# Delta-net: weight loads and splits at a higher priority than the small steps around them

## The chip, the cores and the metric

The kernel runs on one core of a Trainium2 chip. The metric is the device time of one execution in microseconds (us); of several executions the median is taken. The core's engines are PE (TensorE, the matrix products), DVE (VectorE), ACT (ScalarE) and POOL (GpSimd); SP issues the DMAs and works as a queue. PE loads its weights in instructions of their own (PEld) beside the products. TensorE's clock has two levels here, 1.2 and 2.4 GHz; a granted clock of 0.50 in the profile is the lower of them.

## What is computed

One inference step of a trunk of two layers, for 512 tokens of a new prompt and 8 x 4 tokens of samples with a state, 544 columns together, at a width of 1024. Layer 0 mixes by an mLSTM, layer 1 by a gated delta rule, and behind each mixer stands an MLP with a squared ReLU:

```python
for layer in range(DEPTH):                       # 2
    if layer % N_MIXERS == 0:
        y, Cj, nj, mj = mlstm_mixer(x, a_w_in[j], ...)
    else:
        y, Sj, cj = gdn_mixer(x, b_w_in[j], b_conv_w[j], ..., b_w_out[j], S[j], conv[j])
    x = layer_norm(ALPHA * x + y, ln1_g[layer], ln1_b[layer])
    x = layer_norm(ALPHA * x + sq_relu_mlp(x, mlp_w1[layer], mlp_w2[layer]), ...)
```

The change bears on the delta-net mixer:

```python
proj = x @ w_in                                  # 1024 -> 6176 columns
c = silu(conv(proj[..., :CONV_DIM]))             # 4 taps; q, k of 8 heads, v of 16
q = l2norm(q) * DK_B ** -0.5;  k = l2norm(k)
A = M + I                                        # triangle of each head and chunk
sol = triangular_solve(A, rhs)                   # u, w
for each chunk:                                  # the scan, state S
    v_new = u - w @ S;  o = qg @ S + attn @ v_new
    S = gL * S + kdec.T @ v_new
o = head_rms(o) * norm_w * silu(z)
y = o @ w_out                                    # 2048 -> 1024
```

## The kernel before

Activations lie transposed, as tiles of 128 features by 544 columns, in two halves of 272 (`HS`). A weight comes as a tile of 128 outputs: `load_w` takes a raw tile (`wraw`, 128 x 1024, f32, 512 KB), issues its DMA on SP's queue, takes the tiles `wh` and `wl`, and lets `split` make the high part on ACT (a cast, L110) and the low part on DVE (a subtraction, L111). `mm3` multiplies: for each of the 8 blocks k of 128 inputs three products of 128 x 272 in L191, high by high, high by low (`XL`), low (`wl`) by high. The third one of a block is the first to need `wl`. Of `wraw`, `wh` and `wl` there are two buffers each, so the DMA of a tile waits until the split of the tile two before it has read its buffer.

The order of work on every engine is set at build time: each instruction gets a priority when the program text issues it, and among those that are ready with their buffers the scheduler takes the one with the earlier priority. `tc.high_priority(offset=n)` gives the instructions within it a priority n places earlier. Each engine, and SP's queue, then runs its list strictly in order.

The delta-net stage lies at some 690 to 1435 us of the trace. Its weight products run in the sequence `ORDER = "p0 p1 p2 p3 y0 w0 p4 p5 y1 w1 p6 p7 y2 w2 y3 w3"`. A p is `project` for one unit (one head of q and k, two of v): four weight tiles of `wb`, convolution (`conv`: `acc` and `pre`, L983 to L1007, with a sigmoid chain, L507 to L510), transposes and norms. A y is `gate_out` for four heads (`wb` again; the result, split, is `gyh`, `gyl`), a w is the output product with the tiles of `wbo`.

The small work runs beside it in three lanes, each a list of Python generators. `mm3` calls `tick()` behind each block k, and a lane whose period is over makes one step, so that its instructions are issued between products:

- `lane_i`, for each unit: `prepare` makes the triangles (`U`, `A`; L1082 to L1108), brings their 16 x 16 diagonal blocks through DRAM (`dg`, `ub`; L1112, L1117), inverts these on DVE in fifteen steps of two instructions (`tb`, `xb`; L1125, L1127), and sends them back (`dx`, `xc`; L1130, L1132). `invert` builds the inverse of 128 x 128 from them: `DT` (L1156), then short products on PE with an ACT or DVE step behind each (L1164, L1171, L1185, L1193 and L1196, L1205, L1211).
- `lane_s`, the scan over four chunks of 128 tokens (L1243 to L1288), once the inverse is there.
- `lane_d`, for each pair of units the samples: `decode` with the state's tiles `sst` (loads L1294, products of 128 x 8 in L1368), and `update` (products L1419, DVE L1424, stores L1425).

`lanes` is filled at the start of the stage and emptied by `lanes.clear()` at its end; in all other stages it is an empty list.

Of the kernel before, what the change touches and what calls it, by code (L numbers as in the profile page):

```python
# [33 lines left out]
NEG = -1e30  # L34
CLAMP = -40.0
HP = 400
BANKS = (3, 2, 2, 1)
NST = 2
NOT = 6
# [31 lines left out]
def hybrid_kernel(  # L71
# [27 lines left out]
    dma = nc.sync.dma_start  # L99
# [6 lines left out]
    def r32(ap):  # L106
        return ap.bitcast(F32)

    def split(hi, lo, src):
        S.copy(hi, src)  # L110
        V.tensor_tensor(lo, src, r32(hi), op=ALU.subtract)  # L111

    def mtile(tag="a"):
        return pm.tile([P, 512], F32, tag=tag, name="pm_" + tag, bufs=BANKS["gast".index(tag)])

    wide, once = [], []

    def gtile():
# [7 lines left out]
        if tag != "g":  # L126
            return mtile(tag)[:, :HN]
        return pg.tile([P, 512], F32, tag="g", name="pg_t", bufs=BANKS[0])[:, :HN]

# [29 lines left out]
    lanes, done = [], set()  # L159
# [12 lines left out]
    def load_w(src, alloc=None):  # L172

        wn[0] += 1
        pool = wx[0] if wx[0] is not None and wn[0] % 2 else wp
        raw = pool.tile([P, KD, P], F32, tag="wraw", name="wraw", bufs=WBUFS[0])
        dma(raw, src)
        if alloc is None:
            wh = wp.tile([P, KD, P], F32R, tag="wh", name="wh", bufs=WBUFS[1])
            wl = wp.tile([P, KD, P], F32R, tag="wl", name="wl", bufs=WBUFS[2])  # L180
        else:
            wh, wl = alloc()
        split(wh, wl, raw)
        return wh, wl

    def mm3(ps, h, wh, wl, xh, xl, first=True, last=True):
# [30 lines left out]
    def projs(srcs, alloc=None, skip=2):  # L217

        ws = [load_w(src, alloc if i >= skip else None) for i, src in enumerate(srcs)]
        pss = [[None, None] for _ in srcs]  # L220
        for h in range(2):
            for i, (wh, wl) in enumerate(ws):
                pss[i][h] = gtile()
                mm3(pss[i][h], h, wh, wl, XH, XL)
        return pss

    def proj(src, alloc=None):
        return projs([src], alloc, 0)[0]

    wga, w0 = gate_w(0), load_w(wa[0])  # L230
    for j in range(KD):
        dma(XR[j], xT[:, j, :])
# [162 lines left out]
    def out_proj(src, yh, yl, first, ln=None):  # L395

        for jj in range(4):
            wh, wl = load_w(src[jj])
            for u in range(2):
                for h in range(2):  # L400
                    ps = gtile()
                    mm3(ps, h, wh[:, 4 * u:4 * u + 4, :], wl[:, 4 * u:4 * u + 4, :], yh, yl)
                    add_res(2 * jj + u, h, ps, first)
                    if ln:
                        ln.shift(2 * jj + u, h)
# [141 lines left out]
    with tc.tile_pool(name="mc", bufs=1, reuse_waits="tile") as mc, ExitStack() as mx:  # L547
# [313 lines left out]
        for w in ORDER_A.split():  # L861
# [3 lines left out]
            elif what == "s":  # L865
                with tc.high_priority(offset=HP):
                    scan(units[i])
            elif what == "d":
                with tc.high_priority(offset=HP):
                    decode(i, units[2 * i], units[2 * i + 1])  # L870
# [770 lines left out]
```

## Time and profile before

| | us |
|---|---|
| median of 3 runs | 1831.82 |
| the three runs | 1825.68 to 1838.59 |
| the profiled execution | 1825.97 |
| its span | 1824.3 |
| PE busy in it | 1755.2 |
| DVE busy | 1060.5 |
| ACT busy | 827.4 |

The profile shows one execution, on its only core. Times in it count from the start of the span; what lies around the span, 1.7 us, is the difference to the execution's own time. The mean granted clock of PE over the span is 0.968. "Idle before" of an instruction is the time in which its engine stood, and the name behind the arrow the instruction that ended it. A product on PE is pipelined, so the next may start before it ends.

### The profile page before, as it was taken

Reading aid. Unit: us, or ns where it says so; the run is one execution under the profiler, and the core shown is the slowest. Engines: PE = TensorE matmul, PEld = TensorE weight load, DVE = VectorE, ACT = ScalarE, POOL = GpSimd, SP = SyncE. Lnnn points to the kernel's source line nnn. Section 1 sums busy time; section 2 is a strip of 40 time slices with the busy share of each in tenths; the row PEclk is TensorE's granted clock in tenths of the full one; section 3 lists DMA queues with packets and bytes.
Section 4 is the critical chain, followed back from the end, with each engine's and each line's share of the span. In section 5 each row is a group of like instructions: output and inputs, shape, how many; then the busy total and the mean of one; then the engine's idle time right before and its main releaser. Section 6 shows DMA issues by size and latency. Waiting matters only on the chain.

```text
span 1824.3 us, 35692 instructions
## 1 busy us (share of the span) xinstructions
PE 1755.2 (96%) x14580; PEld 1687.1 (92%) x14580; DVE 1060.5 (58%) x2648; ACT 827.4 (45%) x1874; POOL 55.1 (3%) x105
## 2 busy tenths in 40 slices
PE   7999999999999998999899999999999999999997
PEld 7999998999999998889779989998898999999996
DVE  6564767432244368776855877685578643234436
ACT  5444346331234147675643664574346542124314
POOL 2000000000000000011001000000100000000000
PEclk9999999999999999898978999997799999999998
DMA  4122222222223222223314423431232222222311
GB/s 160 58 105 64 71 93 93 71 92 87 88 93 105 82 74 61 56 50 98 111 55 122 123 68 103 130 90 41 79 121 90 90 85 93 82 93 86 111 60 50
DMA packets 84293, 158.88 MB, mean 87 GB/s; under 512 B 37537, under 2 KB 41505, under 8 KB 83617
## 3 DMA queue, kind: packets, MB, share of 16 engines
q1 hardware_dynamic: 84128, 156.60, 27.6%
q8 instruction: 115, 1.88, 0.4%
q14 instruction: 50, 0.40, 0.1%
HBM read 140.51 MB, written 16.06 MB: 86 GB/s over the span
## 4 chain that ended last, share of the span: by engine, by line
PE 81%; DVE 10%; ACT 5%; DMA 2%; issue 1%; POOL 0%; SPq 0%; ACTq 0%; DVEq 0%; POOLq 0%
PE pg_t L191 40%; PE pm_s L191 12%; PE pm_a L191 12%; PE pm_s L1368 2%; DVE lnt L377 1%; DVE lnt L378 1%; PE pm_s L1419 1%; PE pm_s L1254 1%; PE pm_a L1090 1%; PE pm_s L1265 1%; DVE acc L995 1%; ACT wh L110 1%; DVE wl L111 1%; DVE XL L389 1%; PE pm_s L1281 1%
## 5 line engine op out<-in xcount | busy, mean ns | idle before, releaser
L111 DVE TENSOR_TENSOR wl<-wraw,wh 128x1024 fp32r<-128x1024 f32 x200 | 244.7, 1224 | 360.9 <-ACT wh L110 360.3
L191 PE MATMUL pg_t<-XH,wh 128*128 128x272 f32 x1480 | 446.0, 301 | 8.7 <-ACT XH L110 7.6
L191 PE MATMUL pg_t<-XH,wl 128*128 128x272 f32 x1480 | 438.4, 297 | 7.5 <-DVE wl L111 7.5
L191 PE MATMUL pg_t<-XL,wh 128*128 128x272 f32 x1480 | 439.3, 297 | 0.1
L110 ACT CAST wh<-wraw 128x1024 fp32r<-128x1024 f32 (+1 forms) x201 | 210.4, 1047 | 465.4 <-PE pg_t L191 212.4
L191 PEld LDWEIGHTS pg_t<-XH,wh 128*128 128x128 f32 x1480 | 285.3, 193 | 13.0 <-ACT XH L110 7.6
L191 PEld LDWEIGHTS pg_t<-XH,wl 128*128 128x128 f32 x1480 | 284.5, 192 | 10.0 <-DVE wl L111 8.9
L191 PEld LDWEIGHTS pg_t<-XL,wh 128*128 128x128 f32 x1480 | 284.9, 193 | 2.4 <-DVE XL L111 0.4
L191 PE MATMUL pg_t<-h,wh 128*128 128x272 f32 x672 | 129.2, 289 | 0.0
L191 PEld LDWEIGHTS pg_t<-h,wh 128*128 128x128 f32 x672 | 105.6, 188 | 0.3
L191 PE MATMUL pg_t<-h,wl 128*128 128x272 f32 x336 | 96.9, 288 | 0.0
L191 PE MATMUL pm_a<-h,wh 128*128 128x272 f32 x496 | 95.3, 288 | 0.0
L191 PE MATMUL pm_s<-h,wh 128*128 128x272 f32 x496 | 94.9, 288 | 0.0
L191 PE MATMUL pm_s<-XH,wh 128*128 128x272 f32 x288 | 84.1, 292 | 0.0
L191 PE MATMUL pm_s<-XH,wl 128*128 128x272 f32 x288 | 83.7, 291 | 0.0
L393 DVE SCALAR_TENSOR_TENSOR XR<-XR,pg_t 128x272 f32<-128x272 f32 x118 | 51.1, 434 | 56.1 <-PE pg_t L191 55.4
L191 PE MATMUL pm_s<-XL,wh 128*128 128x272 f32 x288 | 83.7, 291 | 0.0
L191 PE MATMUL pm_a<-XL,wh 128*128 128x272 f32 x280 | 82.4, 294 | 0.9 <-DVE XL L389 0.8
L191 PE MATMUL pm_a<-XH,wh 128*128 128x272 f32 x280 | 82.9, 296 | 0.0
L191 PE MATMUL pm_a<-XH,wl 128*128 128x272 f32 x280 | 81.5, 291 | 0.0
L191 PEld LDWEIGHTS pm_s<-h,wh 128*128 128x128 f32 x496 | 77.9, 188 | 0.2
L191 PEld LDWEIGHTS pm_a<-h,wh 128*128 128x128 f32 x496 | 78.0, 188 | 0.1
(573 smaller groups left out, 3924.6 us busy)
## 6 DMA issues: line engine op xcount, KB each, us to landing
wraw<-in_w SPq DMA_DIRECT2D x64, 512.0 KB, 3.5
wraw<-in_wb SPq DMA_DIRECT2D x48, 512.0 KB, 3.5
wraw<-in_w2a SPq DMA_DIRECT2D x32, 512.0 KB, 3.5
sst<-in_s SPq DMA_DIRECT2D x64, 256.0 KB, 3.0
wraw<-in_wa SPq DMA_DIRECT2D x24, 512.0 KB, 3.5
wraw<-in_w2b SPq DMA_DIRECT2D x24, 512.0 KB, 3.4
out_ss<-sst SPq DMA_DIRECT2D x32, 256.0 KB, 3.0
wraw<-in_wbo SPq DMA_DIRECT2D x16, 512.0 KB, 3.8
```

The source lines that it names most:

```text
L110: S.copy(hi, src)
L111: V.tensor_tensor(lo, src, r32(hi), op=ALU.subtract)
L191: T.matmul(ps, lhsT=wt[:, k, :], rhs=xt[k][:, HS[h]], start=first and k == 0 and q == 0, stop=last and k == n - 1 and q == 2,)
L377: V.tensor_tensor(t, x, rs, op=ALU.mult)
L378: V.tensor_tensor(t, t, mu, op=ALU.subtract)
L389: V.tensor_tensor(XL[j][:, HS[h]], x, r32(XH[j][:, HS[h]]), op=ALU.subtract)
L393: V.scalar_tensor_tensor(x, x, ALPHA if first else 1.0, ps, op0=ALU.mult, op1=ALU.add)
L995: V.scalar_tensor_tensor(acc, pre[:, q:q + WC], cw[q], acc, op0=ALU.mult, op1=ALU.add)
L1090: T.matmul(pk[:, q * 256:(q + 1) * 256], lhsT=kq[:, 0, c0:c0 + P], rhs=kq[:, :, c0:c0 + P], start=True, stop=True)
L1254: T.matmul(pks[:, w], lhsT=kq[:, w, cc], rhs=St, start=True, stop=True)
L1265: T.matmul(pv[:, j], lhsT=X[:, 4 * (ch // 2) + 2 * j + ch % 2], rhs=rhs[:, j] if ch else vtok[:, j, 0], start=True, stop=True)
L1368: T.matmul(pkq[:, r], lhsT=t[:, r], rhs=kqf[:, :, o:o + 4], start=True, stop=True)
```

## The change

In `load_w` the DMA of the raw tile is issued behind the allocation of `wh` and `wl` instead of ahead of it, and DMA and split get a priority that is 300 places earlier while there are lanes, 0 places otherwise.

```diff
+AHEAD = 300
...
         raw = pool.tile([P, KD, P], F32, tag="wraw", name="wraw", bufs=WBUFS[0])
-        dma(raw, src)
         if alloc is None:
             wh = wp.tile([P, KD, P], F32R, tag="wh", name="wh", bufs=WBUFS[1])
             wl = wp.tile([P, KD, P], F32R, tag="wl", name="wl", bufs=WBUFS[2])
         else:
             wh, wl = alloc()
-        split(wh, wl, raw)
+
+        with tc.high_priority(offset=AHEAD if lanes else 0):
+            dma(raw, src)
+            split(wh, wl, raw)
         return wh, wl
```

In the changed program the lines of the helpers up to L177 stand one further down and those behind `load_w` three: the cast is L111, the split L112, the load's DMA L185, the product L194, L1164 is L1167.

Order, first place: DVE in the convolutions at 738 to 743 us of the trace, ahead of the first products of a tile of `wb`. Before:

```order
L995 SCALAR_TENSOR_TENSOR acc<-pre,cst,acc 128x568 x4
L507 TENSOR_SCALAR pre<-acc 128x568
L995 SCALAR_TENSOR_TENSOR acc<-pre,cst,acc 128x568
L1107 TENSOR_TENSOR U<-pm_a,Eh 128x256
L507 TENSOR_SCALAR pre<-acc 128x568
L1108 TENSOR_TENSOR A<-pm_a,Eh 128x256
L111 TENSOR_TENSOR wl<-wraw,wh 128x1024
L999 TENSOR_TENSOR acc<-acc,pre 128x512
L1002 TENSOR_TENSOR vsxb<-acc,pre 128x28
```

In the changed program:

```order
L998 SCALAR_TENSOR_TENSOR acc<-pre,cst,acc 128x568 x3
L112 TENSOR_TENSOR wl<-wraw,wh 128x1024
L510 TENSOR_SCALAR pre<-acc 128x568
L998 SCALAR_TENSOR_TENSOR acc<-pre,cst,acc 128x568
L1110 TENSOR_TENSOR U<-pm_a,Eh 128x256
L998 SCALAR_TENSOR_TENSOR acc<-pre,cst,acc 128x568
L1111 TENSOR_TENSOR A<-pm_a,Eh 128x256
L1002 TENSOR_TENSOR acc<-acc,pre 128x512
L1005 TENSOR_TENSOR vsxb<-acc,pre 128x28
```

The split of the weight (`wl`) now stands behind three of the four L995 ahead of it, and a sigmoid step, the other two L995, `U` and `A` follow it.

Order, second place: PE at the inverse of unit 2, behind the products L1193 and L1196, at some 924 us of the trace. Before:

```order
L1196 MATMUL pm_a<-Z_10279,DB 32x32
L191 MATMUL pg_t<-XH_75,wh 128x272
L191 MATMUL pg_t<-XL_83,wh 128x272
L191 MATMUL pg_t<-XH_75,wl 128x272
L191 MATMUL pg_t<-XH_76,wh 128x272
L1205 MATMUL pm_a<-ZX,U 64x64 x8
L191 MATMUL pg_t<-XL_84,wh 128x272
L191 MATMUL pg_t<-XH_76,wl 128x272
L191 MATMUL pg_t<-XH_77,wh 128x272
L191 MATMUL pg_t<-XL_85,wh 128x272
L191 MATMUL pg_t<-XH_77,wl 128x272
L191 MATMUL pg_t<-XH_78,wh 128x272
```

In the changed program (L1199 is L1196, L1208 is L1205, L1214 is L1211):

```order
L1199 MATMUL pm_a<-Z_10279,DB 32x32
L1208 MATMUL pm_a<-ZX,U 64x64 x8
L1214 MATMUL pm_a<-X,ZX 64x64 x8
L1079 MATMUL pm_a<-RE,hmr 128x12 x2
L1093 MATMUL pm_a<-kq 128x256
L1268 MATMUL pm_s<-vtokb,X 128x128 x2
L1093 MATMUL pm_a<-kq 128x256
L1099 LDWEIGHTS identb
L1099 MATMUL pm_a<-maskw,identb 128x512
L1275 MATMUL pm_s<-vd,ktok 128x256
L1284 MATMUL pm_s<-vn,A 128x128 x2
```

The products L191 that stood between the steps of the inverse are gone from here; they stand ahead of the inverse now.

Order, third place: SP's queue at the blocks of unit 2, at 880 to 893 us of the trace. Before:

```order
L177 DMA wraw<-in_wb 128x1024
L1294 DMA sst<-in_s 128x512 x2
L1112 DMA dg<-U 32x4x32 x8
L1425 DMA out_ss<-sst 128x512
L1117 DMA ub<-dg 64x16x16
L1294 DMA sst<-in_s 128x512
L1425 DMA out_ss<-sst 128x512
L1294 DMA sst<-in_s 128x512
L177 DMA wraw<-in_wbo 128x1024
```

In the changed program:

```order
L185 DMA wraw<-in_wbo 128x1024
L1297 DMA sst<-in_s 128x512 x2
L1115 DMA dg<-U 32x4x32 x8
L185 DMA wraw<-in_wbo 128x1024
L1120 DMA ub<-dg 64x16x16
L1428 DMA out_ss<-sst 128x512
L1297 DMA sst<-in_s 128x512
L1428 DMA out_ss<-sst 128x512
L1297 DMA sst<-in_s 128x512
```

Two loads of weight tiles (`wraw`) now stand ahead of `ub`, and one of them between `dg` and `ub`; before, the next load behind that of `in_wb` came four places behind `ub`.

## Rows read from the trace of the kernel before

**Rows 1.** The page, part 1: busy time, share of the span, instructions.

```profile
PE 1755.2 (96%) x14580; PEld 1687.1 (92%) x14580; DVE 1060.5 (58%) x2648; ACT 827.4 (45%) x1874; POOL 55.1 (3%) x105
```

**Rows 2.** Windows: span; busy PE, PEld, DVE, ACT, POOL; clock, DMA share, GB/s.

```profile
735.00:1150.00 415.00, 393.37 (x3873) 363.42 (x3873) 298.31 (x953) 234.51 (x633) 30.47 (x53) 0.93 0.31 88
...
735.00:945.00 210.00, 194.19 (x1856) 176.15 (x1855) 149.83 (x485) 125.97 (x341) 15.70 (x26) 0.90 0.28 79
```

**Rows 3.** PE's waits, 735 to 1150: total us, times, longest.

```profile
PE pg_t L191 <- DVE wl L111: 7.1, 4, 3.4
PE pm_a L1164 <- DVE DT L1156: 4.6, 4, 1.4
```

**Rows 4.** Windows, columns as in rows 2: gaps and stretches at half speed.

```profile
743.20:746.70 3.50, 3.50 (x16) 3.17 (x16) 2.28 (x8) 1.12 (x3) 0.00 (x0) 0.51 0.64 169
...
832.00:835.40 3.40, 3.40 (x18) 3.40 (x17) 1.88 (x6) 0.77 (x4) 0.00 (x0) 0.50 0.60 182
838.80:849.10 10.30, 10.30 (x48) 10.30 (x48) 4.33 (x18) 4.82 (x17) 0.00 (x0) 0.50 0.45 141
902.00:910.50 8.50, 3.46 (x14) 1.97 (x13) 8.09 (x34) 3.41 (x10) 0.00 (x0) 1.00 0.48 155
910.50:934.40 23.90, 22.32 (x289) 19.26 (x290) 5.35 (x13) 5.65 (x12) 3.56 (x8) 0.50 0.30 94
913.80:944.30 30.50, 29.48 (x339) 25.20 (x340) 10.62 (x29) 11.57 (x32) 2.37 (x6) 0.66 0.20 66
972.00:982.20 10.20, 10.20 (x49) 10.20 (x48) 2.35 (x9) 1.16 (x3) 0.00 (x0) 0.50 0.48 147
1084.60:1088.00 3.40, 3.25 (x22) 3.05 (x22) 1.28 (x3) 0.13 (x1) 2.23 (x5) 0.50 0.02 5
```

**Rows 5.** PE's timeline at 838: start, us, instruction [idle before <-releaser].

```profile
838.59 1.47 PE L1368 MATMUL pm_s<-kqx,sst 128*128 128x8 f32 x8
```

**Rows 6.** The tile wraw, 735 to 1150: its splits, ns min/median/max.

```profile
L111 DVE TENSOR_TENSOR wl<-wraw,wh x34: 1184/1215/1307, 741.1 to 1142.1; 128x1024 fp32r<-128x1024 f32 x34
```

**Rows 7.** SP's waits, 690 to 1435: total us, times, longest.

```profile
SPq L177 <- DVE wl L111: 145.6, 25, 30.6
```

**Rows 8.** Timeline of ACT, PE and DVE, 738 to 743.2.

```profile
738.36 1.05 ACT L110 CAST wh<-wraw 128x1024 fp32r<-128x1024 f32 x1 [1.17 <-PE pm_s L191]
...
739.94 0.29 PE L191 MATMUL pg_t<-XL,wh 128*128 128x272 f32 x1
...
741.15 1.22 DVE L111 TENSOR_TENSOR wl<-wraw,wh 128x1024 fp32r<-128x1024 f32 x1
...
742.42 0.39 PE L191 MATMUL pg_t<-XH,wl 128*128 128x272 f32 x1 [2.19 <-DVE wl L111]
```

**Rows 9.** Timeline of ACT and PE, 828 to 832.6.

```profile
828.33 1.06 ACT L110 CAST wh<-wraw 128x1024 fp32r<-128x1024 f32 x1
...
831.75 0.39 PE L191 MATMUL pg_t<-XH,wl 128*128 128x272 f32 x1 [1.19 <-DVE wl L111]
```

**Rows 10.** Timeline of SP, DVE and PE, 905.5 to 919.

```profile
906.22 0.47 SPq L1130 DMA_DIRECT2D dx<-xb  x1
...
909.63 2.34 DVE L111 TENSOR_TENSOR wl<-wraw,wh 128x1024 fp32r<-128x1024 f32 x2
...
913.81 1.05 PE L1164 MATMUL pm_a<-DT,U 32*32 32x16 f32 x64 [1.19 <-DVE DT L1156]
...
915.54 1.05 PE L1171 MATMUL pm_a<-DB,Z 32*32 32x16 f32 x64
```

**Rows 11.** Window of the chain ahead of that, columns as in rows 2.

```profile
889.60:906.20 16.60, 14.80 (x94) 12.54 (x92) 15.30 (x65) 9.32 (x23) 0.95 (x1) 1.00 0.50 166
```

**Rows 12.** SP's timeline, 884 to 914: the loads and ub.

```profile
887.03 0.63 SPq L1117 DMA_DIRECT2D ub<-dg  x1
...
892.74 0.35 SPq L177 DMA_DIRECT2D wraw<-in_wbo  x1
```

**Rows 13.** The chain that ended last: start, us, what.

```profile
887.94 3.02 PE pg_t L191 x24
```

## The prediction

> **What bounds the kernel now.** I began with the busy times: PE works for 96% of the span [rows 1], so time can come only from its gaps, from the clock it is granted, or from work taken off it. The change takes no work off any engine. The switch `AHEAD if lanes else 0` is on only while the lanes hold steps, that is in the delta-net stage, and the order of instructions differs in bulk only between about 735 and 1150 us of the trace (after 1155 PE stands at the same place in both orders, to a few products). In that stretch of 415 us PE is busy for 393.37 us at a mean clock of 0.93; the first half, to 945 us, is the poor one, 194.19 of 210 at 0.90, which leaves 199.18 of 205 for the second [rows 2].
>
> Two things can therefore be won: the 21.6 us in which PE stands, and the half-speed stretches. The list of what PE waited for splits the first: 7.1 us for the low part of a weight tile (`wl`, DVE) in four waits, which is nearly all that concerns weights, against 4.6 us for DT, the first step of a triangle's inverse, also in four waits [rows 3]. The rest is spread over other lane steps. For the second, stretches with a granted clock of 0.50 or 0.51, half of the full 2.4 GHz, hold 3.50 + 3.40 + 10.30 + 22.32 + 10.20 + 3.25 = 53.0 us of busy PE [rows 4], so they cost about 26.5 us against full speed. Three of them begin right behind a wait for a weight (743.2, 832.0 and 910.5); those at 838.8 and 972.0 do not. Ahead of 838.8 the engine was issuing 128x8 state products with no idle before them [rows 5].
>
> **What the change does, part by part.** It adds and removes no instruction. It lets the load, cast and split of a weight pass up to 300 positions of lane work, and by that lets the products that need the weight pass too.
>
> *The casts and splits themselves.* 34 weight tiles are split in the stretch, at 1.215 us of DVE each [rows 6], and none is added. PE waited for four of them [rows 3]; the low parts of the other 30 were there when they were read, and to have those earlier gives PE nothing. The loads can't go much earlier either: in most cases the queue already stands until a split sets a raw buffer free (145.6 us of such standing in 25 waits [rows 7]). So the change can gain only at the few places at which PE did wait, and I take these in turn.
>
> *Place 1, 739 to 747 us.* The cast began at 738.36 and took 1.05 us, so the split could begin at 739.41; it began at 741.15 behind conv and lane work, and PE waited 2.19 us until 742.42 [rows 8]. In the new order the split stands behind the third L995 of the run, ahead of 3.4 us of that work. From 739.41 it ends at 740.6; PE, whose last product without `wl` lasts from 739.94 to 740.23 [rows 8], then waits some 0.4 us, a gain of 1.8. Behind it PE runs 3.50 us at half speed [rows 4]; if the gap goes I count that as given back, 1.75. Place 1: 3.5 us, between 1.8 (the wait alone) and 3.9 (no wait left).
>
> *Place 2, 830 to 835 us.* PE waited 1.19 us until 831.75, with the cast begun at 828.33 and 1.06 us long [rows 9]. In the new order the split is past some 14 us of DVE's inverse steps (L1125, L1127) and can begin at 829.4, so it ends at about 830.6; 1.0 us goes, and with it half of the 3.40 us at half speed, 1.7. Place 2: 2.7 us, between 0 and 2.9. A fourth wait, of 0.3 us at 770, goes too.
>
> *Place 3, 902 to 944 us, unit 2's inverse.* This is the largest: 5.04 us idle in 902 to 910.5, 1.19 at L1164, 1.02 behind it to 944.3, and 22.32 us busy at half speed, which costs 11.2; together 18.4 us [rows 4, 10]. The wait for `wl` in it, 7.1 less the others, is 3.4, and all of that goes: the split that ended it began at 909.63, though its cast had been done long before, and the new order has it past 29 us of DVE work. But DVE isn't free there. It was busy for 15.30 of the 16.60 us in which it ran the chain L1125, L1127 [rows 11], which ends in `dx` (issued 906.22), `xc`, DT, and the products L1164 at 913.81 [rows 10]. Two splits now stand within that chain and make it 2 x 1.21 = 2.4 us later, while PE gets to L1164 3.4 us sooner. The wait there becomes 1.19 + 3.4 + 2.4 = 7.0 us. That is a wait that takes the place of the one removed.
>
> Behind L1164 comes a second loss. Before, 46 products of L191 stood between L1164 and the next product that needs `gyl`, 25 of them between L1164 and L1211, and filled the hops of the inverse; in the new order 7 are left, two of them up to L1211, since the rest went ahead. In the trace L1164 begins at 913.81 and lasts 1.05, and L1171 begins at 915.54 [rows 10]: 0.68 us of hop, under which one product lay. Five such hops of the inverse without cover are 3.4 us; with about three of the scan's steps behind them I put 5.5 us. Bounds: 1.0 (the idle time there now) and 24 (35 hops at 0.68, with no lane covering another). For the half clock I put 10 us of busy PE instead of 22.32, a cost of 5, because less work is left for the stretch behind the gap; bounds are 0 and 11.2. Place 3 afterwards: 7.0 + 5.5 + 5 = 17.5 against 18.4, a gain of 0.9, between a loss of 24 and a gain of 17.
>
> *The queue of loads.* A weight load that is put ahead waits at the head of SP's queue until its raw buffer is free, and what was ahead of it now stands behind it. For six of the eight units one to four weight loads are newly ahead of `ub`, `dx` or `xc`. At unit 2 two loads, the first of them issued at 892.74 before, now stand ahead of `ub`, issued at 887.03 before [rows 12]. If the splits that free the buffers move up with them, this costs nothing beyond the 7.0 above, which is the value I take; the price if not is a rival below.
>
> *ACT and the rest.* Casts that move up pass 0.5 to 11 us of ACT work; ACT is busy for 234.51 of 415 us [rows 2], so I put 0. The half-speed stretches at 838.8, 972.0 and 1084.6 and all of 945 to 1150 I leave as they are. In the stages without lanes the offset is 0, and I put 0.
>
> **Sum.** 3.5 + 2.7 + 0.3 + 0.9 = 7.4 us. The profiled execution took 1825.97 us, which becomes 1818.6; it lies 5.85 below the median of the runs shown, 1831.82, and from the median I take the same 7.4: **1824 us**.
>
> **Rivals.** *(a) Nothing that can be measured, 1832 us.* What places 1 and 2 give is taken by lane steps: DVE and ACT make the same work in another order, and each of the four waits at L1164 (4.6 us now) grows by what PE arrives sooner. For it: place 3 above, where I find just that. Against it: places 1 and 2 have no inverse step waiting right behind.
>
> *(b) The clock stays up, 1798 us.* With products ready ahead of need, PE has no gaps in 735 to 1150 that bring its clock down: 26.5 of half clock and 7.1 of weight waits, 33.6 us. For it: three of the six stretches follow a weight wait. Against it: 838.8 and 972.0 fell without one, and the new order makes a bare run behind L1164. The Trainium skill ("TensorE: Matmul & The Clock Gate", section "What's actually happening") says that the clock follows how busy the engine has been, and that the slow state is the default; by that the result would be (b), and the rows at 743.2, 832.0 and 910.5 agree, while those at 838.8 and 972.0, with PE busy all along, do not.
>
> *(c) Slower, 1855 us.* The loads hold up `ub`, `dx` and `xc`. A weight load waited 145.6 / 25 = 5.8 us on average for a raw buffer [rows 7]. If in four of the six units this wait falls onto the path to L1164, with PE's products spent and a short stretch at half clock behind it like that of 743.2 (1.75), the loss is 4 x (5.8 + 1.75) = 30.2; less 6.5 from places 1 and 2 and 770, 23.7. It decides as soon as the loads' wait is longer than what PE has in products ahead: it runs 30 to 40 products ahead at 825 to 930, 4 to 5 us at 0.125 us each (24 in 3.02 us [rows 13]). For it: the new order of SP. Against it: the splits move up as well. That the change doesn't do what it says (most tiles already had slack) ends in (a).
>
> **How the numbers follow.** Forecast 0.50, (a) 0.25, (b) 0.13, (c) 0.12. 1% of the time, 18 us, is about what a measurement of this kernel can tell from no change, so faster means below 1813.5 and slower above 1850. Faster: (b), and 0.07 of the forecast's case with place 3 near its good end, 0.20. Slower: most of (c), 0.11. Same: 0.69. The range runs from 1802, place 3 at its gain of 17 and some of the other half clock, to 1848, place 3 with its bare run uncovered; it leaves out most of (b) and of (c).
>
> **What the trace of the changed kernel would show.** Waits of PE for `wl` in the stretch under 1 us in all, instead of 7.1. The waits for DT at L1164 up from 4.6 to some 10, with 7 at unit 2, which then stands nearer to 914 than to 910. DVE's chain ahead of that longer by two splits. A short half-clock stretch behind L1164, and those at 743 and 832 gone, that at 838.8 still there. The span from 945 to 1150 as before. I would be wrong on the side of (b) if the mean clock of 735 to 945 rose from 0.90 to 0.97 or more; on the side of (c) if SP shows waits of a weight load with `ub` or `xc` behind it and L1164 waits several us in most units.

## The result, and the profile after

The changed kernel took 1817.38 us (median), the kernel before 1831.82; the ratio of the means is 0.9936 with a 95% interval of 0.9910 to 0.9961, and in a second series 0.9950 (0.9926 to 0.9973). By the ratios that is 9 to 12 us less. Forecast were 7.4 us less, 1824, in a range from 1802 to 1848.

The profiled execution took 1814.86 us, 11.1 less than that of before, with a span of 1813.2. Busy times and the last rows of the page's slices (PE, its granted clock):

```profile
PE 1742.2 (96%) x14580; PEld 1678.0 (93%) x14580; DVE 1062.3 (59%) x2648; ACT 831.2 (46%) x1874; POOL 56.1 (3%) x105
...
PE   7999999999999999899979999999898999999997
...
PEclk9999999999999999899979999997799999999998
```

PE is busy 13 us less than before [rows 1] though it executes the same 14580 products, and 96% of the span as before: what shrank is the time that the products took, not the time in which PE stood. The windows, with borders at the same point of the work (to some 2 us), columns as in rows 2:

```profile
732.10:940.00 207.90, 189.41 (x1870) 175.54 (x1870) 151.97 (x492) 127.82 (x338) 16.64 (x26) 0.90 0.28 80
732.10:1136.00 403.90, 381.11 (x3829) 355.39 (x3830) 298.75 (x958) 236.59 (x628) 31.55 (x52) 0.95 0.31 90
1136.00:1423.70 287.70, 273.58 (x2323) 256.57 (x2323) 208.22 (x579) 156.91 (x380) 9.03 (x19) 0.93 0.30 93
```

The stretch that took 415.0 us [rows 2] takes 403.9. Ahead of it 1.1 us were gained up to 690 and 1.8 at the gates, and the last part of the stage, 285.0 us before, now takes 287.7. In the 403.9 us PE stands for 22.8 us, against 21.6. So of the 7.1 us of waiting for `wl` [rows 3] all but 0.5 are gone, and the idle time is not. The list of what PE waited for from 735 to 1150 us (us in all, times, longest) shows where it went:

```profile
PE pm_a L1167 <- DVE DT L1159: 4.9, 2, 4.3
PE pm_t L1040 <- DVE kq L1002: 3.3, 1, 3.3
PE pm_t L1065 <- DVE acc L1002: 3.1, 2, 2.8
PE pm_a L1099 <- ACT Eh L1107: 1.4, 1, 1.4
...
PE pg_t L194 <- DVE wl L112: 0.5, 1, 0.5
```

What fell is the time at half speed. These are all stretches of the stage with a granted clock of 0.50:

```profile
728.30:735.10 6.80, 6.80 (x33) 6.71 (x32) 3.91 (x13) 3.67 (x14) 0.00 (x0) 0.50 0.07 11
755.60:762.40 6.80, 5.96 (x27) 5.96 (x28) 5.32 (x25) 5.54 (x18) 0.00 (x0) 0.50 0.37 90
837.50:844.30 6.80, 6.80 (x32) 6.80 (x32) 3.83 (x17) 2.69 (x4) 0.00 (x0) 0.50 0.44 135
898.90:902.30 3.40, 3.34 (x10) 2.69 (x11) 2.70 (x14) 0.88 (x4) 0.00 (x0) 0.50 0.37 121
909.20:929.60 20.40, 14.74 (x260) 12.75 (x261) 5.19 (x16) 7.00 (x14) 3.54 (x8) 0.50 0.23 68
1069.60:1073.00 3.40, 3.40 (x17) 3.40 (x16) 1.43 (x4) 0.00 (x0) 1.19 (x2) 0.50 0.05 4
1230.00:1250.50 20.50, 19.74 (x284) 17.33 (x283) 5.43 (x14) 7.58 (x15) 2.93 (x7) 0.50 0.12 44
1281.20:1298.30 17.10, 15.86 (x71) 14.91 (x69) 4.95 (x20) 1.48 (x4) 1.18 (x2) 0.50 0.35 101
1301.70:1305.10 3.40, 3.40 (x75) 2.98 (x73) 0.73 (x2) 0.06 (x1) 1.31 (x4) 0.50 0.14 46
```

Those behind the two first waits for `wl`, at 743.2 and 832.0 [rows 4], are gone, new ones stand at 755.6 and 898.9, and that of 10.2 us at 972.0 is gone, near which no wait for a weight had been. From 732 to 1136 us PE is busy at half speed for 37.3 us (34.2 in the rows from 755.6 to 1073, 3.0 in the end of the first), against 54.4 (53.0 [rows 4] and the end of one that begins ahead of 735): 17 us, worth 8.5 if a microsecond at half speed costs half a microsecond, as the prediction counts it. Idle time costs 1.2 more. The remaining 3.8 of the 11.1 us lie within PE's busy time, in stalls too short to be listed as idle; I did not follow them. (Half is a little too much: in the kernel before, products of 128x272 start 0.126 us apart at full speed, at 965 us, and 0.227 at half speed, at 972.2 to 973.6, so 0.44 is lost. By that the 17 us are worth 7.5.)

### The profile page after: what moved, and what is told of

Same layout as the page of the kernel before. It is cut to its first block, busy times and chain, and to the rows that moved or that the text cites. A ratio compares the mean times of both kernels' runs of the same rounds, so it can differ in the third digit from the quotient of the medians.

```text
span 1813.2 us, 35720 instructions
## 1 busy us (share of the span) xinstructions
PE 1742.2 (96%) x14580; PEld 1678.0 (93%) x14580; DVE 1062.3 (59%) x2648; ACT 831.2 (46%) x1874; POOL 56.1 (3%) x105
## 4 chain that ended last, share of the span: by engine, by line
PE 80%; DVE 10%; ACT 4%; DMA 3%; issue 1%; POOL 1%; SPq 0%; ACTq 0%; DVEq 0%; POOLq 0%
PE pg_t L194 39%; PE pm_s L194 13%; PE pm_a L194 12%; PE pm_s L1371 2%; DVE lnt L380 1%; PE pm_s L1422 1%; DVE lnt L381 1%; PE pm_s L1257 1%; DMA xc<-dx 1%; PE pm_s L1268 1%; PE pm_a L1093 1%; DVE wl L112 1%; DVE acc L998 1%; PE pm_s L1275 1%; DVE XL L392 1%
## 5 line engine op out<-in xcount | busy, mean ns | idle before, releaser
L112 DVE TENSOR_TENSOR wl<-wraw,wh 128x1024 fp32r<-128x1024 f32 x200 | 245.3, 1227 | 370.6 <-ACT wh L111 369.8
L194 PE MATMUL pg_t<-XH,wh 128*128 128x272 f32 x1480 | 443.9, 300 | 3.3 <-ACT wh L111 2.8
L194 PE MATMUL pg_t<-XH,wl 128*128 128x272 f32 x1480 | 437.6, 296 | 1.0 <-DVE wl L112 1.0
L194 PE MATMUL pg_t<-XL,wh 128*128 128x272 f32 x1480 | 438.3, 296 | 0.0
L111 ACT CAST wh<-wraw 128x1024 fp32r<-128x1024 f32 (+1 forms) x201 | 210.1, 1045 | 472.7 <-PE pg_t L194 221.2
L194 PEld LDWEIGHTS pg_t<-XH,wh 128*128 128x128 f32 x1480 | 284.6, 192 | 7.4 <-ACT wh L111 4.5
L194 PEld LDWEIGHTS pg_t<-XH,wl 128*128 128x128 f32 x1480 | 283.8, 192 | 3.1 <-DVE wl L112 1.7
L194 PEld LDWEIGHTS pg_t<-XL,wh 128*128 128x128 f32 x1480 | 284.4, 192 | 2.0
L194 PE MATMUL pg_t<-h,wh 128*128 128x272 f32 x672 | 129.2, 289 | 0.0
L194 PEld LDWEIGHTS pg_t<-h,wh 128*128 128x128 f32 x672 | 105.8, 189 | 0.3
L194 PE MATMUL pg_t<-h,wl 128*128 128x272 f32 x336 | 97.0, 289 | 0.0
L194 PE MATMUL pm_a<-h,wh 128*128 128x272 f32 x496 | 95.3, 289 | 0.0
L194 PE MATMUL pm_s<-h,wh 128*128 128x272 f32 x496 | 95.0, 289 | 0.0
L194 PE MATMUL pm_s<-XH,wh 128*128 128x272 f32 x288 | 84.7, 294 | 0.0
L194 PE MATMUL pm_s<-XL,wh 128*128 128x272 f32 x288 | 84.4, 293 | 0.0
L194 PE MATMUL pm_s<-XH,wl 128*128 128x272 f32 x288 | 84.3, 293 | 0.0
L194 PE MATMUL pm_a<-XL,wh 128*128 128x272 f32 x280 | 82.3, 294 | 0.8 <-DVE XL L392 0.8
L396 DVE SCALAR_TENSOR_TENSOR XR<-XR,pg_t 128x272 f32<-128x272 f32 x118 | 51.0, 434 | 54.4 <-PE pg_t L194 53.9
L194 PE MATMUL pm_a<-XH,wh 128*128 128x272 f32 x280 | 82.6, 295 | 0.0
L194 PE MATMUL pm_a<-XH,wl 128*128 128x272 f32 x280 | 81.3, 290 | 0.0
L194 PEld LDWEIGHTS pm_s<-h,wh 128*128 128x128 f32 x496 | 78.0, 189 | 0.2
L194 PEld LDWEIGHTS pm_a<-h,wh 128*128 128x128 f32 x496 | 78.0, 188 | 0.1
```

Of the source, the lines that this page charges most:

```text
L194: T.matmul(ps, lhsT=wt[:, k, :], rhs=xt[k][:, HS[h]], start=first and k == 0 and q == 0, stop=last and k == n - 1 and q == 2,)
L396: V.scalar_tensor_tensor(x, x, ALPHA if first else 1.0, ps, op0=ALU.mult, op1=ALU.add)
```

## The experiments

Each ran beside the kernel before on one chip, in five rounds. Besides the ratio the table gives, for the one profiled execution, the delta-net stage from the gates' first product (L960) to the first product of MLP 1 that reads `wx`: its length, PE's idle time in it, PE's busy time at a granted clock of about 0.5, and the rest, which is the length less idle time less half of the half-speed time. The three numbers come from windows over the stage and over each half-speed stretch, as for the first row: 697.7 - 662.6 busy = 35.1, and 35.1 + 98.1 / 2 + 613.5 = 697.7. The last column is not of the profiled execution: it is the granted clock over the whole span, as a mean of all executions that the ratio compares.

| kernel | ratio (95%) | stage | idle | half speed | rest | clock |
|---|---|---|---|---|---|---|
| before | 1 | 697.7 | 35.1 | 98.1 | 613.5 | 0.965 |
| load_only | 1.0003 (0.9981 to 1.0025) | 702.1 | 36.1 | 107.1 | 612.6 | 0.965 |
| changed kernel | 0.9936 (0.9910 to 0.9961) | 688.5 | 38.6 | 80.1 | 609.8 | 0.971 |
| after_again (the same) | 0.9950 (0.9926 to 0.9973) | 692.9 | 39.2 | 88.5 | 609.4 | 0.969 |
| split_only | 0.9955 (0.9933 to 0.9978) | 685.8 | 39.7 | 71.3 | 610.5 | 0.969 |
| subtract_only | 0.9983 (0.9965 to 1.0001) | 709.4 | 43.4 | 114.8 | 608.6 | 0.968 |
| project_only | 0.9982 (0.9961 to 1.0003) | 698.9 | 40.4 | 97.0 | 610.0 | 0.968 |
| gate_out_only | 1.0122 (1.0079 to 1.0165) | 720.4 | 44.7 | 126.0 | 612.6 | 0.958 |
| ahead_60 | 0.9933 (0.9901 to 0.9966) | 685.5 | 35.3 | 71.2 | 614.6 | 0.971 |
| ahead_1000 | 1.0132 (1.0096 to 1.0168) | 724.1 | 51.1 | 125.1 | 610.4 | 0.958 |
| chain_up | 1.0036 (1.0015 to 1.0058) | 711.1 | 42.0 | 123.3 | 607.5 | 0.961 |
| spread_before | 0.9964 (0.9939 to 0.9988) | 692.1 | 45.7 | 56.4 | 618.2 | 0.976 |
| spread_60 | 1.0025 (1.0004 to 1.0046) | 707.9 | 46.4 | 92.1 | 615.4 | 0.968 |
| spread_after | 1.0059 (1.0032 to 1.0086) | 709.1 | 51.7 | 90.1 | 612.3 | 0.963 |

The clock column bears on all that follows, since one profiled execution need not stand for its kernel: that of split_only is the fastest of its twelve (1811.82 us, median 1821.78), that of subtract_only the slowest (1837.20, median 1827.41). A mean clock of 0.965 over the 104 executions of the kernel before amounts to some 128 us at half speed in the whole span ((1 - 0.965) x 2 x the span). Among these executions, time and half-speed time go together (correlation 0.96): one microsecond more at half speed comes with 0.39 us more time.

**after_again.** No edit.

> The changed kernel, once more. It gave 0.9936 of the time before. In its first trace, PE's half-speed stretch of 10.2 us at 972 is gone, with no wait near it removed, and those at 743 and 832 are gone behind waits that went. Theory 1: all stretches follow from the order of instructions and its gaps; then this execution has the same list, six stretches between 728 and 1073 us with about 41 us of busy PE, and the ratio is 0.992 to 0.995. Rival: a stretch that no gap starts comes and goes from one execution to the next; then one near 840 or 967 is missing or back, by 5 to 10 us of busy PE, and the executions of the one kernel scatter by 3 to 5 us.

The rival holds, in smaller pieces than expected at 840 and 967. The waits are the same to 0.4 us (DT 3.99 instead of 4.31, kq 3.33 in both), but the half-speed time is 88.5 instead of 80.1 us: the stretch near 966 is back for 3.4 us, the one at 837 is 10 us long instead of 7, and one at 1304 is 14 instead of 3. The executions of this series reach from 1814 to 1833 us.

**load_only.** The load alone is raised:

```diff
         with tc.high_priority(offset=AHEAD if lanes else 0):
             dma(raw, src)
-            split(wh, wl, raw)
+        split(wh, wl, raw)
```

> Only the load of a raw tile is raised by 300 places; cast and split stay where they were. Theory 1 (the gain comes from the DVE subtraction passing lane work; the loads wait for raw buffers anyway): the four waits for wl, 7.1 us, are still there, the delta-net stage is as before, and what is left is the 1 us at the start of the kernel, where a load now stands behind XR0: ratio 0.999, 0.998 to 1.0005. Rival (the gain comes from earlier loads): 0.994.

As theory 1 said: 1.0003, and waits for `wl` of 7.2 us. The order of PE, by line and tile, differs from that of before in 127 of 14580 places only: the loads mostly waited for raw buffers [rows 7], and the splits that free these stayed where they were. The start of the kernel gives nothing either: the gates come at 725.7 us, as before (725.6), while the two executions of the changed kernel have them at 723.6 and 725.9.

**split_only.** Cast and subtraction are raised, the load is not:

```diff
+        dma(raw, src)
         with tc.high_priority(offset=AHEAD if lanes else 0):
-            dma(raw, src)
             split(wh, wl, raw)
```

> Cast and subtraction are raised by 300 places, the load stays at its own priority. Theory 1: the loads follow the raw buffers that the splits free, so the order of almost all instructions is that of the changed kernel, and so is the time: the losses up to the third inverse and to 990 us as in its two traces (some 40 us against 48 before), the two waits for DT near 909 (4 us) and for kq near 753 (3.3 us) as there, ratio 0.992 to 0.9965. Rival (cast and subtraction are worth only what subtract_only gave): 0.9975 to 1.0.

0.9955, with the changed kernel's order of PE in all but 108 places and the same waits (DT 4.37 near 905, kq 3.32 near 751): the split carries the whole change, as far as the two intervals can tell.

**subtract_only.** Only DVE's half of the split is raised:

```diff
         with tc.high_priority(offset=AHEAD if lanes else 0):
-            dma(raw, src)
-            split(wh, wl, raw)
+            V.tensor_tensor(wl, raw, r32(wh), op=ALU.subtract)
```

(The load and `S.copy(wh, raw)` stand ahead of it.)

> Only DVE's subtraction is raised by 300 places; load and cast on ACT stay at their own priority. Theory 1: in the waits for wl the cast had been done before, so the subtraction alone removes them and frees the raw buffers as early: ratio as the changed kernel's, 0.9925 to 0.9955, waits for wl below 1.5 us. Rival (the cast on ACT has to move too): waits for wh take their place, 0.997 to 1.0.

Theory 1 was right on the waits and wrong on the time; the rival's waits for `wh` did not come, but its ratio did. The waits for `wl` are gone and no wait for `wh` took their place; the sixth inverse comes 413.5 us behind the gates, against 416.6 before and 406.9 in the changed kernel, and the rest of the stage takes 295.9 us instead of 281.1. In that rest there are 62 us of PE's busy time at half speed instead of 39. This is the slowest execution of the twelve, though; over all of them the mean clock, 0.968, is above that of before. So these 62 us don't stand for the kernel, and what an earlier cast adds stays open.

**project_only** and **gate_out_only.** The raise for the tiles of one kind of step alone:

```diff
-        with tc.high_priority(offset=AHEAD if lanes else 0):
+        with tc.high_priority(offset=AHEAD if lanes and turn_[0] in 'p' else 0):
```

(and `in 'yw'` for the other; `turn_[0]` holds the kind of step of ORDER.)

> The raise by 300 places only for weight tiles that project loads (the p steps); those of gate_out and of the output product keep their own priority. Theory 1 (the gain is the sum of places): places 1 and 2, at 739 and 830 us, lie in p steps, so their 6 us stay, and the wait for wl near 907, in gate_out, comes back with its 3.4 us; the stretch from the gates to the sixth inverse, 416.7 us before and 406.8 in both traces of the changed kernel, takes 408 to 411, ratio 0.995 to 0.998. Rival (it is the products run ahead of y and w that keep the clock up): 413 or more, ratio 0.998 to 1.0.

> The other half: the raise only for tiles of gate_out and of the output product (y and w steps). Theory 1: the waits for wl at 740 and 830 are there as before, the one near 907 is gone and a wait for DT at unit 2's inverse takes its place, so almost nothing is gained: 413 to 417 us from the gates to the sixth inverse, ratio 0.998 to 1.0005. Rival: 407 to 410, ratio 0.995 to 0.997.

With p alone the waits for `wl` of places 1 and 2 are gone, and the one near 907 did not come back, against theory 1; the stretch to the sixth inverse takes 411.3 us, at its edge, and the ratio of 0.9982 (0.9961 to 1.0003) fits both expectations. PE stands 6.4 us at unit 2's inverse. The sum of places falls with the other half. With y and w alone the time is not the same but 1.2% longer, which neither theory had. There PE stands for the evacuation of gate_out's own products (`sgmz`, L1440), during which a half-speed stretch of 27 us begins. What PE waited for in the stage of gate_out_only:

```profile
PE pg_t L194 <- DVE sgmz L1440: 7.2, 4, 4.6
PE pm_s L1246 <- DVE xb L1130: 4.8, 2, 2.6
PE pm_s L1246 <- DVE go_on L1233: 4.5, 4, 1.9
...
PE pg_t L194 <- DVE wl L112: 2.7, 3, 1.2
```

One half gives 0.2% less and the other 1.2% more, both together 0.5 to 0.6% less: the parts don't add up.

**ahead_60** and **ahead_1000.**

```diff
-AHEAD = 300
+AHEAD = 60
```

(or 1000.)

> The whole change with 60 places instead of 300. Theory 1: the splits that PE waited for passed some 3 to 29 us of DVE work; 60 places are enough for places 1 and 2 but pass less of the inverse chain, so the waits for wl stay below 2 us, the wait for DT at unit 2 is below 3 us instead of 4.3, and the time is that of the changed kernel or up to 3 us less, ratio 0.993 to 0.996. Rival: 60 is too few for place 3, wl near 907 keeps 3 us, ratio 0.996 to 0.999.

> 1000 places instead of 300. Theory 1: nothing is left to win from waits for wl (0.5 us in the changed kernel), and lane steps are passed by more splits: waits for DT, kq and acc grow by 2 to 6 us in all, with half-speed stretches behind them, ratio 0.995 to 0.999. Rival: the more the better, ratio 0.991 to 0.994.

Sixty places give the same as 300, within the intervals, but not by the way I named. The waits for `wl` at places 1 and 2 are still there (2.16 and 1.24 us), and near 912 PE stands 3.16 us for `sgmz`. What PE waited for in the stage of ahead_60:

```profile
PE pg_t L194 <- DVE sgmz L1440: 5.1, 5, 3.2
PE pg_t L194 <- DVE wl L112: 3.7, 3, 2.2
...
PE pm_a L1167 <- DVE DT L1159: 2.3, 3, 0.9
```

The gain is in the clock, 71.2 us at half speed instead of 98.1: no stretch at all at 1240, where the wait for `acc` ahead of it is 1.22 us instead of 2.24, and 3 + 3 + 10 us around unit 2's inverse instead of 24. Its executions reach from 1807 us up to those of the kernel before, so this trace shows one of the better ones. With 1000 places the waits grow that theory 1 named (idle 51.1), with one of 4.74 us for `sgmz` besides, and the half-speed time is 125.1; but a gain of 0.1 to 0.5% was expected, and it is a loss of 1.3%.

**chain_up.** The inverse's small chain raised as well:

```diff
+                with tc.high_priority(offset=CHAIN):      # 300
                     V.tensor_tensor(tv, ub[:, 0:r, r:r + 1]...
                     V.tensor_tensor(xb[:, 0:r, r:16], ...
...
+            with tc.high_priority(offset=CHAIN):
                 dma(dx..., xb...)
                 dma(xc, dx...)
```

> The changed kernel with one more step: DVE's chain of the small inverses (tb, xb) and the DMAs dx and xc are raised by 300 places too, so that they stand level with the splits. Theory 1 (the wait for wl at 907 became one of 4.3 us at the first product of unit 2's inverse, because the chain got two splits into its way): the wait for DT falls below 2 us, and the half-speed stretch of 20 us behind it shrinks; 3 to 8 us less than the changed kernel, ratio 0.989 to 0.992. Rival: the chain now stands ahead of a split, the wait for wl comes back, and the ratio stays at 0.993 or goes up.

The wait for DT at unit 2 went, as meant, and `wl` did not come back; but the scan's steps now stand behind the chain. What PE waited for in the stage:

```profile
PE pm_s L1249 <- DVE go_on L1236: 5.9, 6, 2.5
PE pm_s L1249 <- DVE xb L1132: 5.2, 2, 3.1
PE pm_a L1170 <- DVE DT L1162: 5.2, 4, 3.2
```

The half-speed time rose to 123.3 us, and the kernel is slower than before, by 0.4%: theory 1 was wrong.

**spread_before, spread_60** and **spread_after.** In the samples' lane a step that does nothing behind each group of 128x8 products, in the kernel before, with 60 and with 300 places:

```diff
                 V.tensor_copy(kqs[:, :, o:o + 16]..., pkq)
                 yield
+                yield
```

> The kernel before, with one edit in the lane of the samples: each group of state products of 128x8 (L1368) is followed by a step that does nothing, so that twice as many weight products stand between two groups. Theory 2 (the half-speed stretches at 839 and 972 us, with no idle ahead of them, come from these products standing close together): both are gone or under 4 us in all, instead of 20.5; 5 to 10 us less, ratio 0.9945 to 0.9975. Rival A (they come from something else at these places): both stay, ratio 0.999 to 1.001. Rival B: the lane is done later and gate_out waits for it, ratio 1.002 to 1.01.

> The changed kernel with 60 places instead of 300 and the same edit of the samples' lane. Theory 2: what spreading gives (no stretch near 840 and 970) comes on top of the 0.9933 of 60 places alone, of which only 10.2 + 3.4 us of half speed lie there: 3 to 6 us more, ratio 0.989 to 0.992. Rival: the sum of half-speed time moves to other places, ratio 0.993 to 0.997.

> The changed kernel, 300 places, with the same edit. In its two traces the half-speed stretch near 967 was missing or 3.4 us, and the one at 837 was 7 to 10 us long. Theory 2: only some 4 us are left to gain, ratio 0.991 to 0.995. Rival: as for 60 places, moved and not gone, ratio 0.995 to 1.0.

In spread_before theory 2 holds: no half speed at 839 or 972, where there were 20.5 us of it, with the waits for `wl` at 744 and 835 still in place, and 0.9964. The mean clock of its executions is 0.976, against 0.964 in the 29 of the kernel before in the same series. Half-speed time fell by 41.7 us in all, since 17 of the 20.5 us at 1245 are gone too, which theory 2 did not name; 10.6 us more idle time and 4.7 of rest take back most of it. Two of its windows, over the places in question (the first holds the 3.4 us at half speed behind the wait for `wl`):

```profile
834.00:846.00 12.00, 10.81 (x77) 10.59 (x77) 8.72 (x34) 6.92 (x27) 0.00 (x0) 0.86 0.38 115
966.00:980.00 14.00, 14.00 (x214) 13.68 (x216) 8.04 (x24) 2.47 (x3) 1.64 (x2) 1.00 0.58 176
```

On top of the change the same edit loses: the two stretches are gone or 3.4 us long there too, but PE waits longer (idle 46.4 and 51.7), among others for the samples' last step (`onx`, L1401, 2.47 and 3.54 us) and for `acc` (L1065, 4.75 us in spread_after), and half-speed stretches of 20 to 24 us begin at these waits.

## Why the prediction was right, and where it was not

**Place 1** was forecast to keep a wait of 0.4 us and lose the half-speed stretch at 743. The timeline of the changed kernel at this place, and at the next convolution:

```profile
735.63 1.05 ACT L111 CAST wh<-wraw 128x1024 fp32r<-128x1024 f32 x1 [2.29 <-PE pm_s L194]
736.70 1.23 DVE L112 TENSOR_TENSOR wl<-wraw,wh 128x1024 fp32r<-128x1024 f32 x1 [2.17 <-ACT wh L111]
...
737.98 0.39 PE L194 MATMUL pg_t<-XH,wl 128*128 128x272 f32 x1 [0.50 <-DVE wl L112]
```

```profile
753.85 1.22 DVE L112 TENSOR_TENSOR wl<-wraw,wh 128x1024 fp32r<-128x1024 f32 x1
...
755.70 0.69 DVE L1002 TENSOR_TENSOR kq<-acc,pre 128x512 f32<-128x512 f32 x1
...
756.44 0.90 PE L1040 MATMUL pm_t<-ident,kq 128*128 128x128 f32 x3 [3.33 <-DVE kq L1002]
```

The wait is 0.50 us instead of 2.19 [rows 8], and there is no half speed behind it: 3.4 us gained, 3.5 forecast. But at the next convolution PE stands 3.33 us for `kq` (0.73 before), with a half-speed stretch of 6.0 us of busy PE around the end of it (3.4 in the second execution). That takes 5.6 us back. No split was put ahead of `kq` here. In the kernel before, the split stands at the same place between two steps (L995) of this convolution:

```profile
756.99 1.23 DVE L111 TENSOR_TENSOR wl<-wraw,wh 128x1024 fp32r<-128x1024 f32 x1 [0.16 <-ACT wh L110]
758.13 0.81 DVE L995 SCALAR_TENSOR_TENSOR acc<-pre,cst,acc 128x568 f32<-128x568 f32 x1
758.99 0.69 DVE L999 TENSOR_TENSOR kq<-acc,pre 128x512 f32<-128x512 f32 x1
...
759.74 0.66 PE L1037 MATMUL pm_t<-ident,kq 128*128 128x128 f32 x4 [0.73 <-DVE kq L999]
```

DVE starts `kq` 3.3 us sooner than that (755.70), and PE is there 5.9 us sooner (753.11 instead of 759.01), so PE stands for the difference. The text had it that places 1 and 2 have no inverse step waiting right behind. That is so, but a step of the convolution did; it is this clause that failed, and rival (a)'s mechanism that took place there.

**Place 2** was right: the wait of 1.19 us is gone, and so is the stretch at 832, 2.9 us for the 2.7 forecast. The stretch at 838.8, which I left as it was, is 6.8 us instead of 10.3 in one execution and 10 in the other.

**Place 3** was right in kind. The wait for `wl` became a wait at unit 2's inverse, and its steps stand bare:

```profile
907.28 0.42 SPq L1135 DMA_DIRECT2D xc<-dx  x1
...
907.64 1.23 DVE L112 TENSOR_TENSOR wl<-wraw,wh 128x1024 fp32r<-128x1024 f32 x1 [0.41 <-ACT wh L111]
...
911.99 1.05 PE L1167 MATMUL pm_a<-DT,U 32*32 32x16 f32 x64 [4.31 <-DVE DT L1159]
...
919.19 1.94 PE L1208 MATMUL pm_a<-ZX,U 64*64 64x64 f32 x16 [0.55 <-ACT ZX L1201]
...
921.80 1.43 PE L1214 MATMUL pm_a<-X,ZX 64*64 64x64 f32 x11 [0.68 <-ACT ZX L1210]
```

The wait at L1167 is 4.3 us, not 7.0. The term that was too large is the 2.4 us by which two splits were to delay the chain of `tb` and `xb`. Only one stands in it, as before. First that split of before, then of the changed kernel, and the window of the changed kernel's chain, to be read beside rows 11:

```profile
891.45 1.21 DVE L111 TENSOR_TENSOR wl<-wraw,wh 128x1024 fp32r<-128x1024 f32 x1
...
893.39 1.21 DVE L112 TENSOR_TENSOR wl<-wraw,wh 128x1024 fp32r<-128x1024 f32 x1
...
885.84:904.15 18.31, 16.42 (x94) 14.17 (x93) 16.48 (x70) 9.44 (x27) 0.95 (x1) 0.91 0.48 166
```

The chain takes 18.3 us instead of 16.6, with 21 instead of 16 state updates (`sst`, L1427) in it, but it begins sooner, and ends 180.6 us behind the gates (180.5 before). The inverse begins 188.4 us behind the gates, as before (188.2). PE only came 3 us sooner. The hops behind it cost 0.58 + 0.46 + 0.55 + 0.68 and 1.42 at L1099, with 0.22 at L1188 3.9 us instead of 5.5; the half speed there is 14.7 us of busy PE instead of 10, 7.4 instead of 5. Together 15.6, where 17.5 was forecast; 3.3 us at half speed at 898.9 and 1.1 us more idle time ahead of it take back what that would have gained against 18.4.

**The sum** came out right largely by luck. The places that were to give 7.4 us gave 1.0 in this trace: place 1 lost 2.2 (3.4 less 5.6), place 2 gave 2.9, the wait at 770 gave 0.3, place 3 nothing. What gave the time are terms that the text had as zero: the half-speed stretch at 972 (5.1 us), which went, or nearly went in the second execution, 1.7 at 838.8, and the short stalls. With the 1.2 us more of idle time, the 8.5 of clock and 3.8 of short stalls, the stretch from 735 to 1150 gave 11.1 us in the trace; 7.4 had been forecast. The last part of the stage, put at zero since PE's order is nearly the same there, gave 2.7 us back: idle time of 14.1 us instead of 11.1 (at 1374.7 PE stands 1.92 us at L1246 instead of 0.44, and there are new or longer waits of 0.5 to 0.7 us at L1049, L1167, L194 and L341). The text also took 18 us for the least that a measurement can tell from no change; the ratio's interval reaches only some 5 us to either side.

**The rivals.** (a) is what happened to idle time as a whole: it was not lower in any of the kernels with raised splits (35.3 to 51.7 us against 35.1). (b) did not come, since half-speed time fell by a fifth in one trace and a tenth in the other. (c) did not come with 300 places: no inverse begins more than 0.3 us later behind the gates than before, and load_only takes the time of the kernel before. A loss of 1.3%, about the size of (c), came with 1000 places; PE's waits there are for steps of DVE (`sgmz`, `kq`, `acc`, `xb`). Whether the queue of loads has a part in them I did not follow.

What the experiments settle: the gain needs the raised splits (split_only has it, load_only does not). It is not the removed waits for `wl` as such, since ahead_60 keeps two of them and gains as much, while subtract_only and project_only remove them and gain 0.2%, not clear of nothing. Over all executions, half-speed time in the whole span is some 128 us before, 106 and 113 in the two series of the changed kernel, 115 in split_only and 106 in ahead_60. At 0.39 us for each, an estimate taken over from the kernel before, that is 5 to 9 us of the 8 to 12 gained. So the cause that I can show for more than half of the gain is less time at half speed. The other 3 us or so lie outside it in all four series, and their cause stays open. In subtract_only and project_only half-speed time is lower too (116 and 117 us, worth some 4 us), and some 3 us are gained by the ratios: there nothing is left over. Why a given order has less half-speed time than its neighbour (60 and 300 against 1000, or both halves against each) I can't derive from the order; this stays open.

## What the runs showed of the hardware

The clock falls without an idle gap. Ahead of the half-speed stretch at 972 in the kernel before, PE was busy without a break for 5.1 us, with 32 products of 128x8 among others; at the same place of the changed kernel the same number stands in 5.0 us, and the clock stayed up. In the second execution of the same program it fell there for 3.4 us, so the order alone does not settle it. Windows of before, then of the changed kernel:

```profile
966.80:971.90 5.10, 5.10 (x46) 5.07 (x46) 3.13 (x14) 1.48 (x3) 0.00 (x0) 1.00 0.42 124
```

```profile
961.00:966.00 5.00, 5.00 (x47) 5.00 (x45) 1.31 (x9) 0.43 (x2) 0.00 (x0) 1.00 0.66 203
966.00:976.20 10.20, 10.04 (x137) 9.42 (x137) 5.87 (x18) 3.66 (x10) 1.19 (x2) 1.00 0.62 171
```

That these short products bring it about in the kernel before, spread_before speaks for: with more weight products between the groups both stretches are gone, and the mean clock over its executions is higher (0.976 against 0.964). The edit moves other steps as well, so it is not a proof. The Trainium skill ("TensorE: Matmul & The Clock Gate", section "What's actually happening") ties the clock to how busy the engine has been; here PE's busy time alone, 5.10 of 5.10 us and 5.00 of 5.00, does not tell the one case from the other.

The same program has different half-speed time in two executions, 80.1 and 88.5 us, which is some 4 us of time; the executions of one kernel spread further (1814 to 1833 us), and in the kernel before 0.39 us of that goes with each microsecond at half speed (clock 0.958 to 0.973 in 104 executions). A single trace shows a place's waits to a tenth of a microsecond, but not how often the clock falls behind them.

## What to carry to other kernels

Where PE is busy for 96% of the time, list the half-speed stretches and what stands ahead of each before the waits: here they cost some 40 us of the stage and the waits for weights 7. Where a wait for a weight goes, PE comes sooner to the next small step that it needs, and stands there if that step is not made sooner too; how far to raise has to be measured, since 60 and 300 places gained 0.5 to 0.7% and 1000 lost 1.3%, and the parts of such a change do not add up. Spreading short products that stand in dense groups between long ones is worth a trial: it gained 0.4% in the kernel before and lost on top of the change, where others waited for the lane that issues them. Before a cause is read from one trace, compare its time and clock with those of the kernel's other executions.
